# Log-sum-exp over rows of 1024: all sums checked on chip, with a branch to a second pass

## The chip, the cores and the metric

One of the eight cores of a Trainium2 chip runs the kernel. The metric is the device time of one execution in microseconds (us). Every run told here was in the fast state, with a granted clock of 1.0. Two figures are kept apart throughout: the **time** of a run, and its **span**, which is the stretch from the program's first to its last instruction in the profile. The span of each timed run is told to 0.1 us. What the time has over the span is called **the outside**.

## The reference

```python
x = np.random.randn(32, 512, 1024).astype(np.float32)      # axis = -1
x_max = np.max(x, axis=axis, keepdims=True)
return x_max.squeeze(axis) + np.log(np.sum(np.exp(x - x_max), axis=axis))
```

There are 16384 rows, 128 for each of the 128 partitions. Subtracting the maximum only guards against overflow and underflow. For normal draws exp(x) is harmless, and the kernel before leaves the maximum out.

## The kernel before

Chunks of rows go from memory into a ring of 51 rows per partition. ScalarE takes exponentials, VectorE adds up rows, ScalarE takes logarithms, and one store ends it. The last four chunks are single rows that ScalarE sums itself. These four sums go to PSUM, TensorE's result memory (`late`), the other 124 columns to SBUF, the large on-chip memory (`sums`).

```python
for i, (r, n_dve, parts, by_halves) in enumerate(CHUNKS):
    if i:
        load(i)                       # SyncE: waits for ring space, starts a transfer
    ...
    if i == len(CHUNKS) - 1:          # logs of 43 columns ahead of the last exponential
        take_logs(logged, late_row, sums[:, logged:late_row], *done_before[-LATE])
    nc.scalar.wait_ge(landed[i], 16)
    ...                               # exponentials; VectorE sums rows, in part by halves
    nc.scalar.activation(out=ring[:, s + j], in_=ring[:, s + j], func=Exp,
                         accum_out=total(row + j)).then_inc(act_done, 1)
    ...
take_logs(late_row, NB, late[:, : NB - late_row], dves, acts)
nc.sync.wait_ge(act_done, acts)
nc.sync.dma_start(out=out_v, in_=res).then_inc(stored, 16)
nc.sync.sem_clear(range(used[0], used[-1] + 1))
nc.sync.wait_ge(stored, 16)
nc.sync.sem_inc(stored, -16)
```

The softmax here doesn't subtract the row's maximum and nothing guards it: scores larger than these inputs give would overflow.

## Time and profile before

| | |
|---|---|
| time | 162.56 us (162.43 to 162.59) |
| span of the profiled run | 161.2 us (its own time: 162.52 us) |
| input read | 67.11 MB, mean 417 GB/s |
| VectorE's last sum ends | 158.04 us |
| ScalarE's last logarithm ends | 159.59 us |
| store issued until, landed at | 159.96, 161.18 us |

The memory paces the body, ScalarE's queue decides when the store starts, and the store's flight is the last 1.2 us. During this flight only SyncE still has an instruction to come. The lines that carry this are in the prediction below.

### The profile page before, as it was taken

The page shows a single profiled execution, that of the slowest core. Times are in us where ns is not written, and L with a number is a line of the kernel's source. Part 1 is how long each engine was busy: PE and PEld are TensorE (multiplying, and loading weights), DVE is VectorE, ACT ScalarE, POOL GpSimd, SP SyncE. Part 2 cuts the span into 40 slices and gives each one's busy share as a digit, 9 for nine tenths or more (in the row PEclk, how much of TensorE's full clock was granted, in tenths as well). Part 3 has the DMA queues.
Part 4 walks back from the last instruction along what each step waited for, and adds up shares of the span by engine and source line. Part 5 has one row for each costly group of instructions (what it writes and reads, how often), then busy time and mean ns, then how long its engine had stood idle before and what let it go on. Part 6 is the DMA issues. An engine that isn't in the chain of part 4 may idle for free.

```text
span 161.2 us, 149 instructions
## 1 busy us (share of the span) xinstructions
DVE 121.0 (75%) x46; ACT 115.1 (71%) x40; POOL 0.2 (0%) x4
## 2 busy tenths in 40 slices
DVE  0028000003999999999999699999999999999892
ACT  3170005996079960999419993999199999999995
POOL 0000000000000000000000000000000000000000
DMA  7999699899899899899889999999899999999990
GB/s 260 504 488 488 290 442 520 374 407 520 374 407 520 374 407 520 374 407 520 374 374 455 455 455 439 423 423 423 385 439 430 434 441 413 418 431 415 409 406 32
DMA packets 2592, 67.18 MB, mean 417 GB/s; under 512 B 288, under 2 KB 416, under 8 KB 928
## 3 DMA queue, kind: packets, MB, share of 16 engines
q1 hardware_dynamic: 2592, 67.18, 97.2%
HBM read 67.11 MB, written 0.07 MB: 417 GB/s over the span
## 4 chain that ended last, share of the span: by engine, by line
DMA 48%; DVE 29%; ACT 20%; issue 0%
DMA ring<-in_x_dram 48%; DVE sums L157 29%; ACT ring L137 17%; ACT ring L164 3%; ACT res L108 0%
## 5 line engine op out<-in xcount | busy, mean ns | idle before, releaser
L157 DVE TENSOR_REDUCE sums<-ring 128x8 f32<-128x8192 f32 (+5 forms) x14 | 111.2, 7994 | 37.1 <-ACT ring L137 37.0
L137 ACT ACTIVATE ring<-ring 128x8192 f32<-128x8192 f32 (+6 forms) x18 | 104.4, 5835 | 43.1 <-DMA ring<-in_x_dram 42.9
L144 DVE CUSTOM_DVE_ANT_0 ring<-ring 128x512 f32<-128x512 f32 x16 | 9.9, 686 | 0.0
L164 ACT ACTIVATE ring<-ring 128x1024 f32<-128x1024 f32 x9 | 9.3, 1042 | 0.0
L122 ACT ACT_TABLE_LOAD x1 | 1.3, 1283 | 1.4 <-PEq L70 1.4
L164 ACT ACTIVATION_READ_ACCUMULATOR ring<-ring 128x1 f32 x9 | 1.6, 174 | 0.0
L144 DVE DVE_READ_ACCUMULATOR2_ANT sums<- 128x1 f32 x16 | 1.3, 83 | 0.0
L108 ACT ACTIVATE res<-sums 128x81 f32<-128x81 f32 (+1 forms) x2 | 0.5, 248 | 0.0
L108 ACT ACTIVATE res<-late 128x4 f32<-128x4 f32 x1 | 0.2, 173 | 0.0
L209 POOL MEMSET const-bfloat16-1.0<- 128x1 bf16 x1 | 0.1, 101 | 0.0
L209 POOL MEMSET const-uint8-127<- 128x1 uint8 x1 | 0.1, 101 | 0.0
L209 POOL MEMSET const-float32-0.0<- 128x1 f32 x1 | 0.1, 98 | 0.2 <-issue 0.2
L209 POOL MEMSET const-float32-1.0<- 128x1 f32 x1 | 0.1, 98 | 0.0
## 6 DMA issues: line engine op xcount, KB each, us to landing
ring<-in_x_dram SPq DMA_DIRECT2D x1, 7680.0 KB, 24.4
ring<-in_x_dram SPq DMA_DIRECT2D x1, 7168.0 KB, 28.6
ring<-in_x_dram SPq DMA_DIRECT2D x1, 6656.0 KB, 35.7
ring<-in_x_dram SPq DMA_DIRECT2D x1, 4608.0 KB, 20.3
ring<-in_x_dram SPq DMA_DIRECT2D x2, 2048.0 KB, 16.0
ring<-in_x_dram SPq DMA_DIRECT2D x1, 3584.0 KB, 28.3
ring<-in_x_dram SPq DMA_DIRECT2D x1, 2560.0 KB, 27.3
ring<-in_x_dram SPq DMA_DIRECT2D x4, 512.0 KB, 27.0
```

Source lines behind the costliest of these rows:

```text
L108: nc.scalar.activation(out=res[:, lo:hi], in_=src, func=Ln).then_inc(act_done, 1)
L122: nc.scalar.preload_act_table_set("natural_log_exp_and_others")
L137: nc.scalar.activation(out=ring[:, s + lo : s + hi], in_=ring[:, s + lo : s + hi], func=Exp).then_inc(act_done, 1)
L144: nc.vector.tensor_tensor_reduce(out=ring[:, s + j, : D // 2], in0=ring[:, s + j, : D // 2], in1=ring[:, s + j, D // 2 :], scale=1.0, scal ...
L157: nc.vector.reduce_sum(out=sums[:, row + lo : row + hi], in_=ring[:, s + lo : s + hi], axis=AX).then_inc(dve_done, 1)
L164: nc.scalar.activation(out=ring[:, s + j], in_=ring[:, s + j], func=Exp, accum_out=total(row + j),).then_inc(act_done, 1)
L209: nc = _bacc.Bacc("TRN2", target_bir_lowering=False, num_devices=1)
```

## The change

The sums are now checked. The check counts how many lie at or above 2^-10 and how many at or below 2^20. If the count is not 32768, three engines branch into a second pass that does the work again with the maxima subtracted. GpSimd marks the 124 early columns, VectorE marks the last four, TensorE adds the marks over partitions by a matmul with ones, and VectorE adds the 256 columns of the result. SyncE, ScalarE and VectorE then load the count into a register and branch. The logs of 43 columns also move behind the last exponential. The intent is safety for other data at little cost in time.

```diff
-        if i == len(CHUNKS) - 1:
-            take_logs(logged, late_row, sums[:, logged:late_row], *done_before[-LATE])
 ...
+    nc.gpsimd.wait_ge(dve_done, dves)
+    nc.gpsimd.wait_ge(act_done, done_before[-1 - LATE][1])
+    mark(nc.gpsimd, sums[:, :late_row], 0, early)       # two tensor_scalar of 128x124
+    nc.tensor.wait_ge(early, 3)
+    add_up(0, 2 * late_row)                             # matmul, 248 columns, fp32
+    last_sum = acts
+    take_logs(logged, late_row, sums[:, logged:late_row], *done_before[-1 - LATE])
+    take_logs(late_row, NB, late[:, : NB - late_row], dves, last_sum)
+    nc.vector.wait_ge(act_done, acts)
+    mark(nc.vector, late[:, :LATE], 2 * late_row, marked)
+    nc.tensor.wait_ge(marked, 2)
+    add_up(2 * late_row, 2 * NB)                        # matmul, 8 columns, fp32
+    nc.vector.wait_ge(counted, 2)
+    nc.vector.reduce_sum(out=n_good, in_=good[:1, : 2 * NB], axis=AX).then_inc(known, 1)
     nc.sync.wait_ge(act_done, acts)
     nc.sync.dma_start(out=out_v, in_=res).then_inc(stored, 16)
+    for engine, reg in ((nc.sync, E.SP), (nc.scalar, E.Activation), (nc.vector, E.DVE)):
+        engine.wait_ge(known, 1)
+        engine.reg_load(deciders[reg], n_good)
+        engine.sem_inc(known, 1)
+    with nc.If_ne(deciders, 2 * P * NB):
+        ...                                             # the second pass, three steps
+    nc.end_ifs()
+    nc.sync.wait_ge(known, 4)
     nc.sync.sem_clear(range(used[0], used[-1] + 1))
+    nc.sync.sem_inc(known, -4)
     nc.sync.wait_ge(stored, 16)
```

More of the change, by code (lines that the diff above doesn't have):

```diff
@@ L6 @@
 from concourse._compat import with_exitstack
+from concourse.ordered_engine_set import OrderedEngineSet
 CHUNKS = [
@@ L23 @@
 LATE = 4
+LOWEST, HIGHEST = 2.0**-10, 2.0**20
+STEP = 43
 @with_exitstack
@@ L43 @@
     assert sum(r for r, *_ in CHUNKS) == NB
-    fp32 = mybir.dt.float32
+    fp32, i32 = mybir.dt.float32, mybir.dt.int32
     Exp = mybir.ActivationFunctionType.Exp
     Ln = mybir.ActivationFunctionType.Ln
-    Add = mybir.AluOpType.add
+    Op = mybir.AluOpType
+    Add = Op.add
+    E = mybir.EngineType
     AX = mybir.AxisListType.X
@@ L57 @@
     res = nc.alloc_sbuf_tensor("res", [P, NB], fp32).ap()
+    ones = nc.alloc_sbuf_tensor("ones", [P, 1], fp32).ap()
+    marks = nc.alloc_sbuf_tensor("marks", [P, 2 * NB], fp32).ap()
+    good = nc.alloc_psum_tensor("good", [P, 512], fp32).ap()
+    n_good = nc.alloc_sbuf_tensor("n_good", [1, 1], i32).ap()
+    top, total_g, log_g, res_g = (ring[:, STEP, k * NB : (k + 1) * NB] for k in range(4))
     landed = [nc.alloc_semaphore(f"landed{i}") for i in range(len(CHUNKS))]
@@ L61 @@
     dve_done = nc.alloc_semaphore("dve_done")
+    early = nc.alloc_semaphore("early")
+    marked = nc.alloc_semaphore("marked")
+    counted = nc.alloc_semaphore("counted")
     stored = nc.alloc_semaphore("stored")
-    used = sorted(sem.num for sem in [*landed, act_done, dve_done])
+    known = nc.alloc_semaphore("known")
+    fetched = nc.alloc_semaphore("fetched")
+    act_g = nc.alloc_semaphore("act_g")
+    dve_g = nc.alloc_semaphore("dve_g")
+    used = sorted(sem.num for sem in [*landed, act_done, dve_done, early, marked, counted])
     assert used == list(range(used[0], used[0] + len(used)))
@@ L120 @@
     n_early = len(body.instructions)
+    deciders = nc.alloc_registers("n_good", OrderedEngineSet([E.SP, E.Activation, E.DVE]))
+    nc.gpsimd.memset(ones, 1.0).then_inc(early, 1)
     nc.scalar.preload_act_table_set("natural_log_exp_and_others")
@@ L172, with mark, add_up @@
         done_before.append((dves, acts))
-    take_logs(late_row, NB, late[:, : NB - late_row], dves, acts)
+    def mark(engine, src, at, sem):
+        n = src.shape[1]
+        for bound, op in ((LOWEST, Op.is_ge), (HIGHEST, Op.is_le)):
+            engine.tensor_scalar(
+                out=marks[:, at : at + n], in0=src, scalar1=bound, scalar2=None, op0=op
+            ).then_inc(sem, 1)
+            at += n
+    def add_up(lo, hi):
+        nc.tensor.matmul(
+            good[:1, lo:hi], lhsT=ones, rhs=marks[:, lo:hi], start=True, stop=True
+        ).then_inc(counted, 1)
@@ L175 @@
+    add_up(2 * late_row, 2 * NB)
+    nc.vector.wait_ge(counted, 2)
+    with nc.allow_low_precision(reason="small whole numbers"):
+        nc.vector.reduce_sum(out=n_good, in_=good[:1, : 2 * NB], axis=AX).then_inc(known, 1)
     nc.sync.wait_ge(act_done, acts)
     nc.sync.dma_start(out=out_v, in_=res).then_inc(stored, 16)
+    for engine, reg in ((nc.sync, E.SP), (nc.scalar, E.Activation), (nc.vector, E.DVE)):
+        engine.wait_ge(known, 1)
+        engine.reg_load(deciders[reg], n_good)
+        engine.sem_inc(known, 1)
@@ new lines, with dve @@
+    with nc.If_ne(deciders, 2 * P * NB):
+        acts_g = dves_g = 0
+        def dve(ins):
+            nonlocal dves_g
+            dves_g += 1
+            ins.then_inc(dve_g, 1)
+        for k, lo in enumerate(range(0, NB, STEP)):
+            hi = min(lo + STEP, NB)
+            x_g = ring[:, : hi - lo]
+            top_g = top[:, lo:hi].unsqueeze(2).to_broadcast([P, hi - lo, D])
+            if k:
+                nc.sync.wait_ge(dve_g, dves_g)
+            nc.sync.dma_start(out=x_g, in_=x_v[:, lo:hi]).then_inc(fetched, 16)
+            nc.vector.wait_ge(fetched, 16 * (k + 1))
+            dve(nc.vector.tensor_reduce(out=top[:, lo:hi], in_=x_g, op=Op.max, axis=AX))
+            nc.vector.wait_ge(dve_g, dves_g)
+            dve(nc.vector.tensor_tensor(out=x_g, in0=x_g, in1=top_g, op=Op.subtract))
+            nc.scalar.wait_ge(dve_g, dves_g)
+            nc.scalar.activation(out=x_g, in_=x_g, func=Exp).then_inc(act_g, 1)
+            acts_g += 1
+            nc.vector.wait_ge(act_g, acts_g)
+            dve(nc.vector.tensor_reduce(out=total_g[:, lo:hi], in_=x_g, op=Add, axis=AX))
+        nc.scalar.wait_ge(dve_g, dves_g)
+        nc.scalar.activation(out=log_g, in_=total_g, func=Ln).then_inc(act_g, 1)
+        nc.vector.wait_ge(act_g, acts_g + 1)
+        dve(nc.vector.tensor_tensor(out=res_g, in0=log_g, in1=top, op=Add))
+        nc.sync.wait_ge(dve_g, dves_g)
+        nc.sync.wait_ge(stored, 16)
+        nc.sync.sem_inc(stored, -16)
+        nc.sync.dma_start(out=out_v, in_=res_g).then_inc(stored, 16)
+        nc.sync.sem_clear(range(fetched.num, dve_g.num + 1))
```

## The prediction

> **What bounds the kernel now.** I read four views in this order: the shares, the chain that ended last, the end of the timeline, and what the transfer queue waited for.
>
> ```profile
> DVE 121.0 (75%) x46; ACT 115.1 (71%) x40; POOL 0.2 (0%) x4
> q1 hardware_dynamic: 2592, 67.18, 97.2%
> DMA 48%; DVE 29%; ACT 20%; issue 0%
> ```
>
> 67 MB of input keep the transfer queue busy for 97% of 161.2 us. The body is a relay of loads, exponentials on ScalarE (ACT) and row sums on VectorE (DVE), all paced by the memory. TensorE does no arithmetic and GpSimd (POOL) only writes four constants, so the two engines the change calls on are free. What decides the end is the last piece of the chain (start, length, what):
>
> ```profile
> 122.25 24.71 DMA ring<-in_x_dram
> 146.96 0.02 issue
> 146.98 2.76 ACT ring L137
> 149.74 1.04 ACT ring L164 x2
> 150.78 4.46 ACT ring L137 x2
> 155.24 3.02 ACT ring L164 x6
> 158.25 0.01 ACT res L108
> 158.26 0.01 issue
> 158.28 1.11 ACT ring L164 x2
> 159.39 0.02 issue
> 159.42 0.17 ACT res L108
> ```
>
> From 146.98 on the loads are ahead and ScalarE works without a hole: the end is ScalarE's queue, then the store. The timeline of the last microseconds gives the handoffs:
>
> ```profile
> 157.96 0.08 DVE L144 DVE_READ_ACCUMULATOR2_ANT sums<- 128x1 f32 x1
> 158.09 0.17 ACT L164 ACTIVATION_READ_ACCUMULATOR ring<-ring 128x1 f32 x1
> 158.14 0.24 ACT L108 ACTIVATE res<-sums 128x43 f32<-128x43 f32 x1
> 158.28 1.04 ACT L164 ACTIVATE ring<-ring 128x1024 f32<-128x1024 f32 x1
> 159.22 0.16 ACT L164 ACTIVATION_READ_ACCUMULATOR ring<-ring 128x1 f32 x1
> 159.42 0.17 ACT L108 ACTIVATE res<-late 128x4 f32<-128x4 f32 x1
> 159.62 0.35 SPq L176 DMA_DIRECT2D out_dram<-res  x1
> ```
>
> VectorE is done with its last sum at 158.04, ScalarE with the last logarithm at 159.59. The store is issued until 159.96 and then the program only waits for it, 1.1 us, which is the last row here (who waited, for whom, total, times, longest):
>
> ```profile
> SPq L181 <- SPq L181: 1.1, 1, 1.1
> ```
>
> The span is 161.19; the time told for a run, 162.56, has 1.37 us more, which I take as constant. So between 159.96 and 161.19 there is a shadow of 1.2 us in which any engine may work for nothing. The question is whether the check fits in it.
>
> **What the Trainium skill says.**
> 1. "DMA: Bandwidth & Descriptors", section Latency and other measured facts, gives a tensor_load a floor of about 600 ns. That is the load of a register from memory, which the change adds. The trace of before has none, so it cannot agree or disagree; it is my largest unknown.
> 2. "Advanced Engine Details and Errata", section Control Flow Timing: a branch about 51 ns, compare-and-branch about 108 ns. The trace of before has plain branches between its first barrier (its events end at 0.7 us) and the next drains (0.8 us), so about 0.1 us at most: it agrees.
> 3. "GPSIMD Engine Reference", sections Instruction dispatch and Elementwise: about 1.8 cycles an element at 1.2 GHz for a tight loop, and some 6 us for the first call of a freshly loaded library. No arithmetic of GpSimd is in the trace of before.
> 4. "TensorE: Matmul & The Clock Gate", section Single matmul latency: (219+N)/1.2 ns for one bf16 matmul on a cold array. These are fp32, of which it gives no figure. Again nothing in the trace of before.
>
> **The change, part by part.**
> *Second pass.* Sums of 1024 exponentials of normal draws lie near 1700, well between 2^-10 and 2^20, so the count is 2x128x128 = 32768 and the pass is never entered. Cost: only the jump over it.
>
> *Order of the logarithms.* The log of 43 columns moves from before the last exponential to after it. Before, it took 0.14 us between two exponentials (158.14 to 158.28), and the last log then had to wait for the last accumulator read (159.38). Now the last exponential starts at 158.14 and its read ends at 159.24; the log of 43 starts at about 159.14, while that read is still on its way, and the log of 4 at about 159.28, ending at 159.45. **Gain 0.14 us**; the store should start at 159.48 and land at 161.03. The last input packet ends before 158 (the transfer share is 5% between 157.5 and 158), so the earlier exponential has its data.
>
> *GpSimd's marks.* Two tensor_scalar of 128x124, released at 158.07. Estimate from the skill's page: 124 x 1.8 / 1.2 = 186 ns plus dispatch, so 0.3 to 0.5 us each; done by about 159. The order of instructions shows one more GpSimd instruction in front of their waits, a library reload. It stands behind the first memset and waits for nothing, so it runs at about 1.5 us, 156 us before it is needed. Then a matmul of 248 columns: one bf16 pass would be (219+248)/1.2 = 389 ns; I estimate two to four for fp32, so it ends between 159.4 and 160.2. All this lies beside ScalarE's last exponential, nearly hidden.
>
> *The visible chain.* VectorE's marks wait for the last log although they only need its input. So, one behind another:
> - last log ends 159.45 (above);
> - handoff 0.03 (as 153.44 to 153.47 between ScalarE and VectorE) and two tiny tensor_scalar, which I put at 0.23 together (a ScalarE log of 4 columns took 0.17 alone): 159.71;
> - handoff, weights and an 8-column fp32 matmul, 0.45 (two passes of (219+8)/1.2 = 189 ns, an estimate from the page, and some more): 160.16. Should the long matmul end at 160.2, this one follows at once;
> - VectorE's sum of 256 elements of one partition. From the rows of the sums by shape, 8192 elements took 8679 ns and 3072 took 3353: 1.04 ns an element and 158 ns fixed; 256 x 1.04 + 158 = 424 ns, with handoff 0.45: 160.61;
> - register load on three engines in parallel: 0.6 by the page; I take 0.9, because a floor is seldom met: 161.5;
> - semaphore increment, compare, branch: 0.02 + 0.11 + 0.05, and 0.2 for instructions fetched anew after the jump (my guess): 161.9;
> - SyncE's wait for all three, the clear (64 ns in the trace of before, at 160.0, then hidden under the store), and three semaphore steps of 17 ns: 162.05.
>
> The store landed at 161.03, so its wait is over when SyncE comes to it. End of span 162.05 against 161.19: **+0.86 us**. Time: 162.56 + 0.86 = 163.4. I add 0.3 because every unknown (first GpSimd call, fp32 passes, register load) can err more upwards than downwards: **163.7 us, +0.7%**.
>
> **The rivals.**
> *A. It all fits under the store.* If marks, matmul, sum and load took 1.6 us together instead of 2.05, the check would end with the store's landing; with the logarithms' gain the time would be 162.4 to 162.6. For it: the 1.1 us wait. Against it: the chain has five handoffs between engines, and the clear is now behind it too. I give it 1 in 10.
> *B. GpSimd becomes the bound.* If the library's code comes only with the first call, about 6 us by the page, the marks would end at 164.1 + 0.5, and matmul, sum, load and branch (about 3 us) follow: span near 168, time near 169, slower by 4%. For it: the reload is there. Against it: it is issued 156 us early. A milder form, cold code costing 1 to 2 us at the first call, gives 164.5 to 165.5.
> *C. The reload steals bandwidth.* The queue is 97.2% busy. If the library is some hundred KB, that is 0.5 us or so at the measured 417 GB/s, and the whole relay shifts. The slack is small: ScalarE starts the last exponential 0.4 us after the last input packet. It would add 0 to 1 us at the end, and be seen as a later first or second landing.
> *D. The register load is slow* (2 us rather than 0.9). Time 164.8.
>
> **Range and chances.** C and D each add about a microsecond to 163.7 at worst, A takes one away. So 162.9 to 165.4 should hold 8 in 10. The 2% line is 165.8 us; only B in its full form, or B's mild form with D, crosses it: 0.09. Faster by 2% is impossible, as 67 MB still have to come in: 0.01. Within 2%: 0.90.
>
> **What would show it.** Logs: the last exponential starts at 158.14, the last log ends near 159.45. GpSimd: marks between 158.1 and 159.1 (B: a long first one). TensorE: the 8-column matmul starts when VectorE's marks end near 159.7 (if it waits for the 248-column one, the GpSimd leg was the longer). Register load: the gap between the end of VectorE's 256-element sum, near 160.6, and SyncE's clear, which I put at 1.3 us. First landings: first exponential at 7.39 us and the second at 25.82 as before (C: later). Store: its wait no longer ends the program. The prediction is wrong if the clear comes before the landing (A), or if GpSimd's first marks end after 160 (B).

## The result, and the profile after

| | before | changed |
|---|---|---|
| time, median of 4 runs | 162.57 us | 163.82 us (163.65 to 164.29) |
| spans | 161.2 (profiled run) | 161.6, 161.7, 161.8, 162.2 |
| time less span | 1.32 | 2.05 to 2.09 |

The ratio of times is 1.0082, 95% interval 1.0059 to 1.0104: 0.8% slower. All ratios here are the mean time of one kernel's fast runs over that of the other's of the same rounds, so not quite the ratio of the medians quoted.

The profiled run of the changed kernel is the one with the span of 162.2. Its second chunk reached ScalarE at 26.33 us instead of 25.82, and everything after it is later by 0.51 us: VectorE's last sum ends at 158.55 instead of 158.04. Below it is read from that point on. First its shares, and the chain that ended last by engine:

```profile
PE 1.0 (1%) x4; PEld 0.3 (0%) x4; DVE 121.6 (75%) x49; ACT 115.0 (71%) x40; POOL 1.3 (1%) x7
q1 hardware_dynamic: 2592, 67.18, 96.9%
DMA 48%; DVE 32%; ACT 16%; POOL 1%; PE 1%; issue 0%
```

The body is what it was. ScalarE's share of the chain fell and GpSimd and TensorE appear in it: the chain now leaves ScalarE before the end. Its last pieces (start, length, what):

```profile
158.56 0.07 issue
158.63 0.52 POOL marks L197
159.15 0.08 issue
159.23 0.53 POOL marks L197
159.76 0.04 issue
159.81 1.04 PE good L203 x4
160.85 0.02 issue
160.87 0.41 DVE n_good L223
```

Note that the chain runs over GpSimd's marks and both matmuls to VectorE's last sum, and does not pass through the logarithms. The timeline of the same stretch shows why:

```profile
159.73 0.23 ACT L128 ACTIVATE res<-sums 128x43 f32<-128x43 f32 x1
159.81 0.09 PEld L203 LDWEIGHTS good<-marks,ones 128*1 128x1 f32 x2 [159.81 <-POOL marks L197]
159.81 1.02 PE L203 MATMUL good<-marks,ones 128*1 128x248 f32 x4 [159.81 <-POOL marks L197]
159.86 0.17 ACT L128 ACTIVATE res<-late 128x4 f32<-128x4 f32 x1
160.06 0.35 SPq L226 DMA_DIRECT2D out_dram<-res  x1
160.07 0.23 DVE L197 TENSOR_SCALAR marks<-late 128x4 f32<-128x4 f32 x2 [1.52 <-ACT res L128]
160.35 0.08 PEld L203 LDWEIGHTS good<-marks,ones 128*1 128x1 f32 x1 [0.46 <-DVE marks L197]
160.59 0.13 PEld L203 LDWEIGHTS good<-marks,ones 128*1 128x1 f32 x1 [0.16 <-issue]
160.87 0.41 DVE L223 TENSOR_REDUCE n_good<-good 1x1 int32<-1x256 f32 x1 [0.57 <-PE good L203]
```

Each matmul as written is two weight loads and two matmuls in the trace, so an fp32 matmul takes two passes. VectorE's small marks end at 160.30. TensorE is still in the long matmul then, and the small one is not done before 160.83. Then come the register loads and the branches (duration in ns, minimum, median and maximum; ScalarE's two lines are left out, they are as long as SyncE's):

```profile
L230 SPq TENSOR_LOAD <-n_good x1: 461/461/461, 161.3 to 161.3; - x1
L230 DVEq TENSOR_LOAD <-n_good x1: 546/546/546, 161.3 to 161.3; - x1
...
L267 SPq COMPARE_BRANCH  x1: 45/45/45, 161.8 to 161.8; - x1
L267 DVEq COMPARE_BRANCH  x1: 67/67/67, 161.9 to 161.9; - x1
```

SyncE clears semaphores at 162.01, and its last instruction ends at 162.23. From the end of the last logarithm (160.04) to the end of the span are 2.19 us, against 1.61 in the kernel before (159.59 to 161.19). One line has no counterpart before. It is the transfer queues' view of the stretch from 161.6 to 164 us, in which the kernel before has no packet at all (packets, MB, share):

```profile
q14 instruction: 1, 0.01, 1.0%
```

It is one packet of 8192 bytes of instructions at 163.12 us, 0.9 us after the program's last instruction.

So the 1.25 us between the medians have two parts: about 0.55 inside the span (median 161.75 against 161.2) and about 0.7 outside it (2.06 against 1.32, rounded spans). The prediction has only the first.

### The profile page after: what moved, and what is told of

Read it like the earlier page. It is cut to its first block, busy times and chain, and to the rows that moved or that the text cites. A ratio compares the mean times of both kernels' runs of the same rounds, so it can differ in the third digit from the quotient of the medians.

```text
span 162.2 us, 173 instructions
## 1 busy us (share of the span) xinstructions
PE 1.0 (1%) x4; PEld 0.3 (0%) x4; DVE 121.6 (75%) x49; ACT 115.0 (71%) x40; POOL 1.3 (1%) x7
## 4 chain that ended last, share of the span: by engine, by line
DMA 48%; DVE 32%; ACT 16%; POOL 1%; PE 1%; issue 0%
DMA ring<-in_x_dram 48%; DVE sums L177 31%; ACT ring L157 16%; DVE ring L164 1%; POOL marks L197 1%; PE good L203 1%; ACT ring L184 1%; DVE n_good L223 0%; DVE sums L164 0%
## 5 line engine op out<-in xcount | busy, mean ns | idle before, releaser
L197 POOL TENSOR_SCALAR marks<-sums 128x124 f32<-128x124 f32 x2 | 1.0, 522 | 157.2 <-DVE sums L164 157.1
L203 PE MATMUL good<-marks,ones 128*1 128x248 f32 (+1 forms) x4 | 1.0, 394 | 159.8 <-POOL marks L197 159.8
```

What stands on the lines that cost most here:

```text
L197: engine.tensor_scalar(out=marks[:, at : at + n], in0=src, scalar1=bound, scalar2=None, op0=op).then_inc(sem, 1)
L203: nc.tensor.matmul(good[:1, lo:hi], lhsT=ones, rhs=marks[:, lo:hi], start=True, stop=True).then_inc(counted, 1)
```

## The experiments

Twelve kernels ran. Theories: **J**, the taken jump makes an engine fetch instructions anew after the end. **L**, the programs have become longer. **G**, GpSimd's library or TensorE's work costs something in closing. **W**, an engine that works late has a closing part that used to be hidden. **T** came last: what counts is *when* an engine gets to the border of a fetched part.

### No branch

Lines from the `If_ne` to `end_ifs()` deleted.

```diff
-    with nc.If_ne(deciders, 2 * P * NB):
-        ...
-    nc.end_ifs()
```

> The whole check stays, to the three register loads, but compare, branch and second pass are gone (wrong only for data out of range). Of the 1.25 us that the change cost, about 0.55 lies inside the span (161.75 against 161.2) and about 0.72 outside it: time less span is 2.06 in the changed kernel and 1.32 in the kernel before. Theory J (the taken jump makes an engine fetch its instructions anew after the end): outside falls to 1.32, span 161.6, time 162.95. Theory L (the programs have become longer, and the end lies in a part that is fetched late): outside falls to 1.32 as well, because the second pass goes with the jump. Theory G (what costs outside is that GpSimd's library is loaded, or that TensorE now works): outside stays 2.06, time 163.65.

163.28 us, ratio 1.0024 (1.0006 to 1.0043); time less span 1.71 to 1.80, no late packet. The expectation missed twice. First, the three register loads are not in the trace: nothing used the registers any more and the build dropped them. So marks, matmuls and sums run here without loads and branch. The inside then costs nothing: from the last logarithm's end (160.30) to the end of the span (161.91) it is 1.61 us, as in the kernel before, because the check ends while the store is still in flight.

```profile
160.32 0.35 SPq L226 DMA_DIRECT2D out_dram<-res  x1
160.33 0.23 DVE L197 TENSOR_SCALAR marks<-late 128x4 f32<-128x4 f32 x2 [1.54 <-ACT res L128]
161.12 0.41 DVE L223 TENSOR_REDUCE n_good<-good 1x1 int32<-1x256 f32 x1 [0.56 <-PE good L203]
```

VectorE's sum ends at 161.53 and the store lands at 161.89, so the check up to the sum fits into the flight. In the changed kernel the loads and branches that follow the sum carry the end past the landing. Second, the outside went down by 0.3 only, to neither 1.32 nor 2.06. No theory had that. It is not explained by length either: built again, the programs of this run have 59, 53 and 33 instructions (VectorE, ScalarE, SyncE), fewer than those of the short jump below, whose outside is 1.33.

### The kernel before, padded

```diff
+    for engine, n in ((nc.vector, 31), (nc.scalar, 14), (nc.sync, 18)):
+        for _ in range(n):
+            engine.nop()
```

> The kernel before with empty instructions on VectorE (31), ScalarE (14) and SyncE (18) early, where these engines wait anyway, so that each has as many as in the changed kernel; no check, no jump. Theory L: time less span rises from 1.32 to 2.06 and the time to 163.3, with an unchanged span of 161.2. Theories J and G: 1.32 and 162.57, nothing changes.

162.74 us, ratio 0.9999, time less span 1.29 to 1.38. **This run is void.** The built programs turned out as long as before (VectorE 55 instructions, ScalarE 52, SyncE 31): empty instructions are dropped. It says only that two equal programs take the same time.

### Early marks on VectorE

```diff
-    nc.gpsimd.wait_ge(dve_done, dves)
-    nc.gpsimd.wait_ge(act_done, done_before[-1 - LATE][1])
-    mark(nc.gpsimd, sums[:, :late_row], 0, early)
+    nc.vector.wait_ge(dve_done, dves)
+    nc.vector.wait_ge(act_done, done_before[-1 - LATE][1])
+    mark(nc.vector, sums[:, :late_row], 0, early)
```

> The changed kernel with the marks of the 124 early columns on VectorE, right after its last sum, instead of on GpSimd. Two of 128x124 should take about 0.3 us each there and end some 0.6 us earlier than GpSimd's (1.12 us for the pair). My theory for the inside: TensorE's long matmul then ends before VectorE's small marks, and the small matmul ends 0.15 to 0.2 us earlier (0.53 us after the small marks in the changed kernel, 0.35 here), so the span is 0.15 to 0.2 shorter. Rival: the small matmul is only slow by itself, and nothing is gained. Outside: G says 1.32 if the library is what costs; J and L say 2.06.

163.56 us, ratio 1.0044 (1.0026 to 1.0061); time less span 2.02 to 2.08. The timeline of its end:

```profile
158.16 0.36 DVE L197 TENSOR_SCALAR marks<-sums 128x124 f32<-128x124 f32 x2
158.58 0.98 PE L203 MATMUL good<-marks,ones 128*1 128x248 f32 x2 [158.58 <-DVE marks L197]
159.68 0.23 DVE L197 TENSOR_SCALAR marks<-late 128x4 f32<-128x4 f32 x2 [1.16 <-ACT res L128]
159.97 0.19 PE L203 MATMUL good<-marks,ones 128*1 128x8 f32 x2 [0.41 <-DVE marks L197]
```

The pair of marks takes 0.36 us on VectorE against 1.12 on GpSimd, and TensorE is free when the small marks are ready. The small matmul ends 0.25 us after them (159.91 to 160.16), against 0.53 in the changed kernel; from the last logarithm to the end it is 1.91 us instead of 2.19. So GpSimd was on the path, and for 0.28 us, more than the 0.15 to 0.2 expected. The outside and its late packet stay without any work on GpSimd beyond small fills: G in its library form is out.

### GpSimd's marks alone in the kernel before

```diff
+    nc.gpsimd.wait_ge(dve_done, dves)
+    nc.gpsimd.wait_ge(act_done, done_before[-1 - LATE][1])
+    ...                               # two tensor_scalar of 128x124, used by nobody
+    nc.sync.wait_ge(early, 2)         # ahead of the clear
```

> The kernel before plus GpSimd's two marks alone, which nobody uses and which end before the store is issued. Theory G in its library form: time less span rises to 2.06, time 163.3. Theories J and L: 1.32, time 162.57. Inside: the rival of the prediction that the library takes bandwidth from the loads would show as a first or second exponential later than 7.39 and 25.82 us; I expect the first to be the same and the second to vary by up to 0.5 us from run to run in either kernel.

162.62 us, ratio 0.9985 (0.9967 to 1.0003); time less span 1.28 to 1.33; the first two exponentials start at 7.45 and 25.92 us. Loading the library cost nothing that these runs can measure, outside or in bandwidth. Across the runs the second start lies between 25.6 and 26.3 us with no relation to the library, and the 26.33 of the profiled changed kernel is one of these.

### VectorE, then ScalarE, made to end late

```diff
+    nc.vector.wait_ge(stored, 16)     # in the second kernel nc.scalar
+    nc.vector.sem_inc(seen, 1)
     nc.sync.wait_ge(stored, 16)
+    nc.sync.wait_ge(seen, 1)
```

> The kernel before with one addition: VectorE also waits for the landing of the store and tells SyncE so, and does nothing else. In the kernel before VectorE has been done since 158.04 and only SyncE is awake until 161.19. Theory W (each engine has a closing part of its own after its last instruction; it was hidden for the engines that finish early, and that of VectorE is longer than SyncE's): from the run without the jump, VectorE's last instruction at 161.59 and a time of 163.66 give 2.07 us for it, so here 161.2 + 2.07 = 163.3 us, time less span 1.95. Theory J alone (the jump is all that costs outside): nothing changes, time less span 1.33, time 162.6 to 162.8.

> The same with ScalarE in place of VectorE. Theory W in the form that any late engine costs as much: 163.3 us. In the form that VectorE is the slow one to close: ScalarE between 1.33 and 2.07, time 162.6 to 163.2.

162.64 us (ratio 1.0012, 0.9995 to 1.0029) and 162.92 us (1.0028, 1.0011 to 1.0045); time less span 1.32 to 1.40 and 1.36 to 1.43. VectorE or ScalarE ending late adds at most 0.1 us to the outside. **W falls.** It had been built on the 1.75 of the run without the branch.

### A short jump

The second pass replaced by one empty instruction per engine, wrong for other data. (Since the build drops those, nearly nothing is left to jump over.)

```diff
     with nc.If_ne(deciders, 2 * P * NB):
-        ...                           # the second pass
+        for engine in (nc.sync, nc.scalar, nc.vector):
+            engine.nop()
```

> The changed kernel with the second pass replaced by one empty instruction on each of the three engines, so check, register loads, compare and jump stay but the jump passes over two instructions, not over 10 to 25. If the late packet of instructions (8192 bytes, 0.9 us after the span's end, in both traces that have the jump and the second pass and in none without) comes of jumping far: no such packet, time less span about 1.75 to 1.85, time 163.3. If any taken jump costs it: packet there, 2.06, time 163.6 to 163.8. Inside: as in the changed kernel, 2.19 us from the end of the last logarithm to the end.

163.08 us, ratio 1.0038 (1.0021 to 1.0055); time less span 1.29 to 1.36, no late packet. Register loads, compare and a taken branch are all there, and the inside is that of the changed kernel: 2.16 us from the last logarithm's end (159.54) to the end of the span (161.71). The outside is that of the kernel before. So **with this check and this jump, all of the 0.7 goes with the second pass's instructions**, though none of them is executed. TensorE and GpSimd work here as in the changed kernel, so G falls in its other form too. One result speaks against a simple reading: the run without the branch lacks the second pass as well and kept 0.4 of the 0.7. Left are J in the form "a far jump", and L.

### A faster check

Everything that the changed kernel does, with a shorter way to the count.

```diff
-    late = nc.alloc_psum_tensor("late", [P, 512], fp32).ap()
+    late = nc.alloc_sbuf_tensor("late", [P, LATE], fp32).ap()
 ...                                   # marks and ones in bf16; early marks on VectorE
+    nc.vector.reduce_sum(out=marks_end[:, :1], in_=marks[:, : 2 * late_row], axis=AX)
+    nc.vector.wait_ge(act_done, last_sum)          # not the logarithms
+    mark(marks_end, late[:, :LATE], 1, marked)
+    nc.tensor.matmul(good[:1, : 1 + 2 * LATE], lhsT=ones, rhs=marks_end, ...)
+    nc.vector.reduce_sum(out=n_good, in_=good[:1, : 1 + 2 * LATE], axis=AX)
```

The four late sums had to leave PSUM. There VectorE's marks and ScalarE's logarithm would read one bank with nothing to order them. The Trainium skill, "Advanced Engine Details and Errata", section Bank Collisions, says that engines cannot use one bank within the same partition in the same cycle; no run here shows it. It is the likely reason why the changed kernel lets the marks wait for the logarithms.

> A shorter check that does all the changed kernel does: early marks on VectorE and summed there to one column while it waits, marks in bf16, the last four sums in SBUF so that they can be marked while ScalarE takes logarithms, one matmul of 9 columns, a last sum of 9 elements. From the last accumulator read: marks 0.26, matmul 0.2, sum 0.2, load and branch 0.7, so the engines are free 1.4 us after it, before the store lands. Span as in the kernel before (161.2 to 161.4). Theory W: VectorE then ends some 0.5 us before SyncE, and the time is about 162.9 to 163.1. If only the length of the check counted, the time would be that of the kernel before.

163.30 us, ratio 1.0051 (1.0034 to 1.0067); time less span 1.94 to 1.97.

```profile
159.29 0.25 DVE L199 TENSOR_SCALAR marks_end<-late 128x4 bf16<-128x4 f32 x2 [0.55 <-ACT ring L186]
159.52 0.35 SPq L230 DMA_DIRECT2D out_dram<-res  x1
159.69 0.17 PE L217 MATMUL good<-marks_end,ones 128*1 128x9 bf16 x1 [159.69 <-DVE marks_end L199]
159.89 0.15 DVE L222 TENSOR_REDUCE n_good<-good 1x1 int32<-1x9 f32 x1 [0.35 <-PE good L217]
```

The count is known at 160.05 us and all branches are done at 160.78, before the store lands: 1.61 us from the last logarithm to the end, exactly the kernel before's, spans 161.1 to 161.4. After the last logarithm the check now costs nothing inside the span, and the time is still up by 0.5%, most of it outside (1.96 against 1.33, which is 0.63 of the 0.79 us between the medians). The late packet is there, at 162.13 us, 1.0 us after the end.

### Length without a jump, and a jump with more length

Real semaphore increments as padding, which the build keeps. The first kernel is the one before, as long as the changed one, with VectorE and ScalarE both ending late; the second is the fast check with 64 more on each of three engines; in the third only VectorE's program is longer.

```diff
+    def longer(name, n):
+        for _ in range(n):
+            getattr(nc, name).sem_inc(spare[name], 1)
+    longer("scalar", 8)               # 64 in the second, 0 in the third
+    longer("vector", 16)              # 64, 16
 ...
+        if i == 3:
+            longer("sync", 10)        # 64, 0
```

> The padding of the second run was void: the compiler drops empty instructions, and the built programs were as long as the kernel before's (VectorE 55, ScalarE 52, SyncE 31 instructions; the changed kernel has 72, 60, 42, the one with the short jump 62, 56, 36). Here the kernel before is made as long as the changed kernel with real semaphore increments early (72, 60, 42), and VectorE and ScalarE also wait for the store, so that no engine's ending is hidden. No check, no jump. Theory L (the length of the programs decides whether the instructions after the end are fetched late): time less span 1.95 to 2.06, a late packet of instructions, time 163.3. Theory J (the far jump does it): 1.33 to 1.43 as with both engines late, no packet, time 162.6 to 163.0.

> The fast check with 64 more real instructions on each of the three engines, executed early where they wait anyway (VectorE 140, ScalarE 124, SyncE 106). Theory L: the border between two fetched parts now falls into the body, where its fetch is hidden, so the late packet goes and time less span falls from 1.96 to about 1.35: time 162.6, no slower than the kernel before, although the program is longer. Theory J: the jump is as far as before, so time less span stays at 1.96 and the time 163.2.

> As the first of this batch, but only VectorE's program is longer (72, 53, 32). Theory L with VectorE as the engine concerned: 1.95 to 2.06. Theory L with ScalarE or SyncE: 1.35 to 1.45. Theory J: 1.35 to 1.45.

| | instructions (VectorE, ScalarE, SyncE) | time | ratio | less span | packets of instructions after the start |
|---|---|---|---|---|---|
| first | 72, 60, 42 | 162.95 | 1.0027 | 1.35 to 1.43 | 147.6 us |
| second | 140, 123 (not 124), 106 | 162.96 | 1.0028 | 1.30 to 1.36 | 9.1, 11.2, 111.6 us |
| third | 72, 53, 32 | 163.00 | 1.0033 | 1.36 to 1.41 | 147.7 us |

The second has the jump over the whole second pass and an outside like the kernel before's, so **J falls: the jump as such costs nothing outside**. The first is as long as the changed kernel and has an outside like the kernel before's, so L falls as well in its plain form. What fits both is T. Every packet of instructions counted here has 8192 bytes, and in these three kernels the packets come in mid-run. In the third kernel only VectorE's program was lengthened, and one packet is there: I take it to be VectorE's. By T, padding put early brings the fetch into mid-run, where other work hides it; in the changed kernel the second pass carries VectorE to it at the very end, where nothing hides it. Where in a program the fetch starts is not shown: in the first and third kernel the packet comes after VectorE's 48th recorded instruction, while the fast check's VectorE ran 61 recorded ones and had its packet only after the end. The queues' view of the third kernel from 147 to 148.5 us has the packet among the loads:

```profile
q1 hardware_dynamic: 52, 0.64, 102.9%
q14 instruction: 1, 0.01, 1.4%
```

These three kernels have spans of 161.5 to 161.9 where the kernel before had 160.9 to 161.3 on that chip. The first and third carry a second handshake after the store (0.1 us in their traces). The rest, about 0.2 to 0.3 us, lies in when loads land, and I did not separate it.

### The fast check with VectorE alone longer

```diff
-    longer("scalar", 64)
-    longer("vector", 64)
+    longer("vector", 24)
 ...
-            longer("sync", 64)
```

> The fast check with 24 more real instructions on VectorE alone, early (VectorE 100, ScalarE 60, SyncE 42). So far: the far jump with a longer program costs nothing outside the span (1.30 to 1.36), so the jump as such is not the cause; a program of the changed kernel's length without the jump costs nothing either (1.35 to 1.43) and shows its packet of instructions at 147.6 us, in mid-run, also where VectorE alone is longer. Theory T (each program is fetched in parts; the packet that VectorE needs for its last instructions and what follows is fetched when it gets there, and is hidden if that is in mid-run, exposed if it is after the end): time less span about 1.33, a packet in mid-run and none after the end, time 162.6 to 162.9, no more than 0.2% over the kernel before. If it is ScalarE's or SyncE's packet that comes late in the fast check: 1.96, late packet still there, time 163.3.

163.27 us, ratio 1.0041 (1.0025 to 1.0057); time less span 1.69 to 1.75. The packet moved from 162.13 to 146.2 us, as T said of VectorE, and nothing comes after the end in the trace. But the outside fell by 0.24 us only, from 1.96 to 1.72, not to 1.33, and the time missed the expected 162.6 to 162.9. So T is right about the packet and accounts for a part of the time only. The remaining 0.4 us is as large as in the run without the branch (1.75), which has no late packet either; whether it is the same thing is not shown. It is absent where ScalarE's and SyncE's programs were longer too (1.33), but there VectorE had 64 more instructions and not 24, so this does not tell which program matters. No packet in the trace belongs to it.

## Why the prediction was right, point by point

The time was right, 163.82 against 163.7, but by luck: the inside cost 0.33 us less than forecast, the 0.3 us added for unknowns was not needed, and about 0.7 us came from outside the span, where the prediction had nothing.

**The step that failed** is "the time told for a run, 162.56, has 1.37 us more, which I take as constant". (The 1.37 sets the median of other runs against the span of the profiled one; that run's own time of 162.52 gives 1.33.) In the changed kernel it is 2.06. With the second pass taken out behind the same check and jump it is 1.33 again, so the extra goes with instructions that are never executed. In the fast check, which has 0.63 us of it, 0.24 went when VectorE's packet was moved into mid-run (1.96 to 1.72); in the changed kernel itself no run moved the packet. The other 0.4 stays open. It does not follow the lengths of the programs alone: the run without the branch has it (1.75) with shorter programs than the short jump's (1.33), and the first padded kernel lacks it (1.35 to 1.43) with the same 60 and 42 instructions on ScalarE and SyncE as the fast check with VectorE alone longer (1.72).

**The inside** was predicted at +0.86 us and is +0.53 from the last sum on (162.23 less the later arrival of 0.51, against 161.19). Its terms, predicted and measured:

| term | predicted | measured |
|---|---|---|
| gain by moving the logs, last sum to last log | 0.14 | 0.06 (1.55 to 1.49) |
| handoff and small marks | 0.26 | 0.26 |
| small matmul | 0.45 | 0.53 |
| handoff and sum of 256 | 0.45 | 0.45 |
| handoff and register load | 0.9 | 0.59 (load 0.46 to 0.55) |
| from the end of VectorE's load to the end | 0.54 | 0.36 |

The register load was the large miss. I had taken it above the skill's floor; it lay below. The logs gave less than thought: between the last two exponentials 1.14 us became 1.07, not 1.00. The small matmul took longer than the estimate because the long one was not done, which the prediction had as a possibility ("Should the long matmul end at 160.2, this one follows at once"). GpSimd's marks took 0.52 us each, just above the estimate of 0.3 to 0.5. So "nearly hidden" was wrong of them: the run with the early marks on VectorE shows that they cost 0.28 us.

**The 0.3 added for unknowns** was meant for GpSimd, passes and register load. Together they did not need it; the outside did. The sum came right for a reason that the prediction did not have.

**The rivals.** A (it fits under the store) did not happen. The run without loads and branch shows that marks, matmuls and sums do fit; the fast check shows that all of it can fit, and that fitting is then not enough. B did not happen: GpSimd's first marks took 0.522 us and its second 0.521, so no first-call cost is left 157 us after the library was asked for at 1.5 us. C did not happen: the run with GpSimd's marks alone is as fast as the kernel before. D did not happen: the load took 0.46 to 0.55 us, less than the 0.9 assumed and not 2.

No version beat the kernel before, and none is expected to: the check only adds. Of those that keep the whole check and its second pass, the fast check with longer programs is the nearest to it, 0.28% over (0.12 to 0.45), against 0.82% (0.59 to 1.04) for the changed kernel.

## What to carry to other kernels

Here a check that ended within the flight of the last store added nothing to the end of the span, so read that flight from the profile first and move everything that can be done earlier (early marks, partial sums) in front of it. Compare the time with the span in every run: code that is never executed can still cost time after the last instruction, and the spans alone do not show it. When padding a program to test its length, count the instructions that were built, because empty ones and unused register loads vanish.

## What the Trainium skill lacked or had wrong

- "DMA: Bandwidth & Descriptors", section Latency and other measured facts, has about 600 ns as the floor of a tensor_load. Here a load of one register from SBUF took 461 ns on SyncE and ScalarE and 546 ns on VectorE (513 to 519 and 547 ns in the fast check).
- "Advanced Engine Details and Errata", section Control Flow Timing, has about 108 ns for compare-and-branch. Here it took 45 ns on SyncE and ScalarE and 67 to 72 ns on VectorE.
- "TensorE: Matmul & The Clock Gate", section Single matmul latency, gives bf16 only. Here an fp32 matmul was two weight loads and two matmuls: 0.98 us for 248 columns, and 0.19 us for 8 columns when TensorE was free (the profiler models the ends of matmuls).
- "GPSIMD Engine Reference", section Instruction dispatch, warns of some 6 us at the first call after a library load. With the load issued at 1.5 us and the first call at 158.6 us, nothing of it was left (522 ns, then 521 ns). It does not say when the cost is hidden.
- "Runtime: NRT & Kernel Launch", section Instruction fetch mechanics, names a taken branch out of the fetched window as a stall and calls the crossing of a border mostly hidden. Here a jump over the same second pass cost nothing outside the span with a longer program (1.33 us) and 0.6 us more with a shorter one (1.96 us): the time at which VectorE's packet is fetched was part of it (0.24 us), and 0.4 us stayed unexplained. No page says that the time after a kernel's last instruction differs between kernels (1.28 to 2.09 us here).
